# x1 transposed into the output, the last addition done onto it, and the sums and weight lows around it moved: one change to a streaming-encoder block

## The chip, the cores and the metric

The kernel runs on one core of a Trainium2 chip. The metric is the device time of one execution in microseconds (us). The kernel before was run three times: 2151.98, 2153.35 and 2154.61 us, median 2153.35. One further execution was recorded by the hardware profiler; its own time is 2155.38 us and the span from its first to its last instruction is 2153.6 us. The engines are called by the profile's names: PE is TensorE (PEld its weight loads), DVE is VectorE, ACT is ScalarE, POOL is GpSimd, SP is SyncE, which here only issues DMAs.

## The reference

One residual block over 2048 tokens of 1024 channels in float32, cut to what matters:

```python
h = rmsnorm(x, norm_mix_pre)
proj = h @ w_in                        # pool branch 512 | GLU 2*512 | gates 1024 + 1024
branch_a = pool_mixer(u_pool, ...)     # trailing means, per-group map, projection
branch_b = conformer_conv(u_glu, ...)  # GLU, causal depthwise conv, LayerNorm, swish, projection
merged = sigmoid(g_a) * branch_a + sigmoid(g_b) * branch_b
x = x + rmsnorm(merged @ w_o, norm_mix_post)          # called x1 below
h = rmsnorm(x, norm_mlp_pre)
f = square(relu(h @ w_up)) @ w_down                   # w_up 1024 x 4096, w_down 4096 x 1024
x = x + rmsnorm(f, norm_mlp_post)
# rmsnorm(x, g) = x * rsqrt(mean(x*x) + 1e-6) * g, over the 1024 channels of a token
```

The change lies in the last three lines and in what feeds them.

## The kernel before, in words

**Tiles and blocks.** The 2048 tokens are two blocks (b) of 1024, each of two halves (t) of 512 tokens. A half has four row groups (g) of 128 tokens. Almost every tile is 128 x 1024 float32, 512 KB. Up to the MLP's square, channels lie on the partitions and tokens along the row; x1 is stored in DRAM in that layout as tiles `x1d[b, c, t]` of two times 128 channels. The MLP's down projection turns this round: its results have tokens on the partitions and channels along the row, in two column halves of 512 (m).

**Products.** Each float32 operand is split into a high part (a cast on ACT) and a low part (source minus high, on DVE), and a product takes three passes, high x high, high x low and low x high. Matrix products are done in a scheme with seven products instead of eight, numbered 1 to 7, whose operands are sums and differences of quarters of the weights and of the activations. A `down` product for one number, one block and one row half h is 24 matmuls of 128 x 512 (line 1708).

**Stages.** Input projection, pooling and convolution branches, merge, output projection, then for each block the up products (`mlp_up`, eight octets), then the down products. The down stage goes over four slabs of the hidden dimension (s = 0 to 3), in each over the seven numbers and the two blocks: a job (s, i, b) is two products (h = 0, 1). Slabs 0 to 2 add into accumulators `acc`. In the last slab the order is: numbers 2, 1, 6, 7, 4 for both blocks, then 5 and 3 for block 0, then 5 and 3 for block 1, so that block 0 is done two jobs earlier. In the last four jobs each job brings its own weights.

**Order of the work.** TensorE's products are the main line. Everything else at its side runs in lanes: generators that are stepped by `bg()` once after each product (lines 1388 to 1420). A lane of rate r takes up to r steps per call; `yield n` makes the lane wait n calls. What a lane issues is ordered behind the main-line instruction last marked at that point. Weights and token cells are requested with a priority that puts them ahead of the main line. Each engine runs its instructions in a fixed order, so an instruction that waits holds back all behind it on that engine, DMA issues on SP and POOL too.

**What the change touches.**

- *Scale of the MLP's inner norm.* The second norm's factor never multiplies the up products; instead its square is folded into the epsilon of the last norm. That needs the mean square of x1 per token. `mlp_scale` (line 1312) computes it during block 1's up products: it loads the 16 tiles `x1d`, squares them on ACT, adds them on DVE, and sums over the partitions by small matmuls with one column (`root_acc`, line 458); `floor[b, t]` is the result.
- *Turning x1 round.* `turned` (line 1771) runs in the first three down slabs in a lane of rate 2: it loads quarters of x1 on POOL's queue, transposes 32 x 32 blocks on DVE (line 1785) and writes them, four DMAs of 128 KB each, into a DRAM tensor `x1t[b, t]` (tokens x channels).
- *Lows of the last slab's weights.* `last_weights` (line 1570) runs in the up stage: for all 14 weight tiles of the last slab it builds the sum or difference, stores the sums (`wsum`), splits them and stores the low parts (`lows`). In the last slab `weights_down(LAST)` (line 1609) loads a tile, casts the high part (line 1647) and loads the low part from `lows`, 18 times.
- *Finish.* `Finish` (line 1799) is one object per (b, t). As the four accumulators of a half become ready, `gain` takes their square sums on ACT (line 1812) and multiplies them by the norm's gain on DVE (line 126). When all are ready, `root` makes the factor r per token, `fetch` loads x1's rows from `x1t`, `cell` does x1 + r * y on DVE, two multiply-adds of 128 x 512 for each row group (line 1832), and `put` writes the row group to the output (line 1839). Three of the four halves do this in `steps`, one after the other in one lane. The last one, (1, 1), does its first half of columns in `last_steps` and the rest in `at_end`, called between the matmuls of the very last products (h = 0, then h = 1): `arrive` adds the product, takes squares and multiplies by the gain, and once both of a product's row groups have arrived, `leave` does the multiply-add with x1's rows and writes each half row (lines 1887 and 1888).

Of the kernel before, what the change touches and what calls it, by code (L numbers as in the profile page):

```python
# [15 lines left out]
P = 128  # L16
D = 1024
# [45 lines left out]
def f32(ap):  # L63
    return ap.bitcast(F32)
# [3 lines left out]
def block_kernel(  # L68
# [124 lines left out]
    fd, x1t = {}, {(b, t): dram("x1t", (T, D)) for b in range(NB) for t in (0, 1)}  # L193
# [958 lines left out]
    floor = {}  # L1152
# [158 lines left out]

    def mlp_scale(b, buf):

        st = None
        for t in (0, 1):
            sq = Squares(buf)
            for c in range(0, CPS, 2):
                x = [mk(*buf) for _ in (0, 1)]
                for i in (0, 1):
                    load(x[i], x1d[b, c + i, t])  # L1320
                yield 1
                sq.add(x[0])
                sq.add(x[1])
            yield 1
            ss = sq.total()
            yield 2
            if st is None:
                st = root_psum()
            root_acc(st, ss, inv_d, t * G)
        yield 1  # L1330
        m = small("sa", 2 * G)
        nc.vector.tensor_scalar(
            m, st[:, : 2 * G], EPS, SQ * EPS**0.5, op0=ALU.add, op1=ALU.mult
        )
        e = p_const.tile([P, 2 * G], F32, tag=f"e{b}", name=f"e{b}")
        mul(e, m, m)
        for t in (0, 1):
            floor[b, t] = e[:, t * G : (t + 1) * G]
        yield
# [230 lines left out]
    def last_weights():  # L1570
# [11 lines left out]
        keys = [(o, i) for o in (0, 1) for i in DOWN]  # L1582
        for (o, i), got in ahead_by_one(keys, fetch_one):
# [15 lines left out]
            hi, lo = split(t, *TR)  # L1599
            yield 1  # L1600
            lows[i, o] = dram("lows")
            load(lows[i, o], f32(lo))

    def scales():
        for b in range(NB):
            yield from mlp_scale(b, (p_fo, "fo"))


    def weights_down(s):
# [27 lines left out]
        def part(i, o):  # L1637
            with tc.high_priority(offset=AHEAD):
# [7 lines left out]
                hi, lo = mk(p_wh, "wh", F32R), mk(p_wl, "wl", F32R)  # L1646
                nc.scalar.copy(hi, t)
                load(f32(lo), lows[i, o])
                return hi, lo
# [120 lines left out]

    def turned():
        for b in range(NB):
            for t in (0, 1):
                to = x1t[b, t].rearrange("(n tb i) (q k j) -> n q i tb k j", n=2, i=32, q=4, j=32)
                for c in (0, 2):
                    for n in (0, 1):
# [7 lines left out]
                        yield 4  # L1784
# [9 lines left out]
                        yield  # L1794

# [3 lines left out]
    class Finish:  # L1799
# [254 lines left out]
```

## Time and profile before

| what | value |
|---|---|
| median of three runs | 2153.35 us |
| profiled execution | 2155.38 us, span 2153.6 us |
| mean granted TensorE clock | 0.996 |
| POOL busy | 74.8 us, 131 instructions |
| SP's queue | 490.93 MB, 63.4% of 16 engines' span |
| ACT's queue | 46.14 MB, 5.5% |
| POOL's queue | 29.37 MB, 3.9% |
| HBM read, written | 370.71 MB, 195.65 MB |

How to read the lines that follow. A row of the busy table by stage gives the stretch, its length, then for PE, PEld, DVE, ACT and POOL the busy us with the number of instructions in brackets, the granted clock, the DMA share and GB/s. A row of the wait table gives the engine and line, what it waited for, the total us, how often and the longest. A row of a group gives line, engine, operation, out<-in, shape and count, then busy us and the mean ns of one, then the idle time before them and its releasers. A row of the timeline gives start, duration, engine, line and operation; "x8" means eight merged. A DMA row gives the queue that issued, the count, the size of one and the median us from issue to landing. The DMA issues before that the change touches:

| transfer | queue | count | KB each | median us to landing |
|---|---|---|---|---|
| fo<-x1d (for the scale) | SP | 16 | 512 | 5.8 |
| tr<-x1d (to be turned) | POOL | 32 | 256 | 3.4 |
| x1t<-tr | POOL | 64 | 128 | 6.1 |
| big<-x1t | SP | 16 | 512 | 7.1 |
| fo<-w_down | SP | 18 | 512 | 6.7 |
| lows<-tr | SP | 14 | 512 | 5.3 |
| wl<-lows | SP | 18 | 512 | 5.2 |
| out<-big | SP | 4 | 512 | 5.0 |

### The profile page before, as it was taken

What the parts mean: (1) busy time and instruction counts of PE and PEld (TensorE: products, weight loads), DVE (VectorE), ACT (ScalarE), POOL (GpSimd) and SP (SyncE); (2) the same over time, 40 slices, a digit from 0 to 9 for tenths busy, and PEclk for the clock granted to TensorE, in tenths of its full rate; (3) what the DMA queues carried; (4) which work ended last, traced back from release to release, by engine and by line L of the source; (5) the groups of instructions that cost most, each with busy time, mean ns of one, the idle gap of its engine ahead of it and who ended that gap; (6) DMA issues with size and microseconds to landing.
All of it is one profiled execution on the core that took longest, in us unless ns stands there. A gap on an engine that the chain in (4) does not pass through costs nothing.

```text
span 2153.6 us, 24989 instructions
## 1 busy us (share of the span) xinstructions
PE 2130.3 (99%) x9424; PEld 1758.8 (82%) x9424; DVE 1717.0 (80%) x1669; ACT 1024.5 (48%) x1109; POOL 74.8 (3%) x131
## 2 busy tenths in 40 slices
PE   9999999999999999999999999999999999999997
PEld 8788888888888888888888888888888888888886
DVE  8999788999779999998768766876745667688558
ACT  6444453334534755446645676665544322223343
POOL 0000000000000000000000000000011111100000
PEclk9999999999999999999999999999999999999999
DMA  4789999688897787335596787995977657564568
GB/s 178 262 309 329 342 356 317 223 292 290 307 345 282 248 305 292 149 118 223 200 382 211 248 293 268 338 334 192 366 264 264 246 197 253 180 221 164 198 228 338
DMA packets 164617, 568.04 MB, mean 264 GB/s; under 512 B 19984, under 2 KB 24208, under 8 KB 164496
## 3 DMA queue, kind: packets, MB, share of 16 engines
q1 hardware_dynamic: 142736, 490.93, 63.4%
q10 hardware_dynamic: 12672, 46.14, 5.5%
q0 software_dynamic: 9088, 29.37, 3.9%
q8 instruction: 74, 1.21, 0.2%
q14 instruction: 47, 0.39, 0.1%
HBM read 370.71 MB, written 195.65 MB: 263 GB/s over the span
## 4 chain that ended last, share of the span: by engine, by line
PE 85%; DVE 8%; DMA 3%; issue 2%; ACT 1%; SPq 0%; DVEq 0%; ACTq 0%
PE up L252 28%; PE down L1708 26%; PE wo L252 7%; PE glu L252 4%; PE B L252 4%; PE gb L252 4%; PE A L252 4%; PE ga L252 3%; DVE y L910 3%; PE pool L252 3%; PE rb L1708 1%; DVE tr L120 1%; DVE wl L123 1%; DMA kept<-ws 1%; PE rb L458 1%
## 5 line engine op out<-in xcount | busy, mean ns | idle before, releaser
L252 PE MATMUL up<-big,wh 128*128 128x512 f32 x1792 | 481.0, 390 | 1.4 <-DVE big L123 0.8
L252 PEld LDWEIGHTS up<-big,wh 128*128 128x128 f32 x1792 | 335.7, 188 | 72.5 <-DVE big L123 1.1
L209 ACT CAST wh<-wr 128x1024 fp32r<-128x1024 f32 x167 | 175.6, 1052 | 305.8 <-PE up L252 70.0
L910 DVE SCALAR_TENSOR_TENSOR y<-v,cst,y 128x1024 f32<-128x1024 f32 x240 | 307.1, 1280 | 2.4
L1708 PE MATMUL down<-wh,fo 128*128 128x512 f32 x756 | 290.3, 389 | 0.3 <-DVE st L120 0.3
L1708 PE MATMUL down<-wh,tr 128*128 128x512 f32 x744 | 289.4, 389 | 0.0
L252 PE MATMUL up<-big,wl 128*128 128x512 f32 x896 | 276.0, 389 | 0.0
L209 ACT CAST wh<-ws 128x1024 fp32r<-128x1024 f32 x124 | 130.6, 1053 | 212.7 <-PE up L252 73.8
L1708 PE MATMUL down<-wl,fo 128*128 128x512 f32 x740 | 227.8, 389 | 0.0
L252 PEld LDWEIGHTS up<-big,wl 128*128 128x128 f32 x896 | 168.1, 188 | 35.0
L123 DVE TENSOR_TENSOR wl<-ws,wh 128x1024 fp32r<-128x1024 f32 x116 | 141.6, 1220 | 48.5 <-ACT wh L209 46.9
L1688 ACT CAST fo<-tr 128x1024 fp32r<-128x1024 f32 x86 | 89.9, 1052 | 176.8 <-DMA tr<-fd 121.0
L1708 PEld LDWEIGHTS down<-wh,fo 128*128 128x128 f32 x756 | 141.9, 188 | 30.4 <-issue 0.9
L1708 PEld LDWEIGHTS down<-wh,tr 128*128 128x128 f32 x744 | 139.6, 188 | 28.9
L1708 PEld LDWEIGHTS down<-wl,fo 128*128 128x128 f32 x740 | 138.9, 188 | 28.9
L123 DVE TENSOR_TENSOR wl<-wr,wh 128x1024 fp32r<-128x1024 f32 x111 | 135.2, 1219 | 25.6 <-ACT wh L209 22.6
L123 DVE TENSOR_TENSOR tr<-tr,fo 128x1024 fp32r<-128x1024 f32 x86 | 103.8, 1221 | 56.4 <-ACT fo L1688 55.9
L120 DVE TENSOR_TENSOR big<-big,down 128x1024 f32<-128x1024 f32 (+1 forms) x79 | 94.0, 1190 | 60.4 <-PE down L1708 60.0
L252 PE MATMUL gb<-big,wh 128*128 128x512 f32 x448 | 121.6, 393 | 0.0
L252 PE MATMUL glu<-big,wh 128*128 128x512 f32 x432 | 117.5, 393 | 3.2 <-ACT tr L408 3.2
L252 PE MATMUL wo<-big,wh 128*128 128x512 f32 x448 | 120.2, 390 | 0.0
L252 PE MATMUL ga<-big,wh 128*128 128x512 f32 x448 | 119.7, 389 | 0.0
(208 smaller groups left out, 3423.9 us busy)
## 6 DMA issues: line engine op xcount, KB each, us to landing
tr<-fd SPq DMA_DIRECT2D x110, 512.0 KB, 5.7
wl<-kept SPq DMA_DIRECT2D x67, 512.0 KB, 4.8
kept<-wl SPq DMA_DIRECT2D x66, 512.0 KB, 5.7
wr<-w_up SPq DMA_DIRECT2D x64, 512.0 KB, 4.6
wr<-w_down SPq DMA_DIRECT2D x62, 512.0 KB, 4.7
wr<-w_in SPq DMA_DIRECT2D x56, 512.0 KB, 5.6
fd<-tr ACTq DMA_DIRECT2D x54, 512.0 KB, 3.7
fd<-tr SPq DMA_DIRECT2D x48, 512.0 KB, 3.1
```

Of the source, the lines that this page charges most:

```text
L120: return nc.vector.tensor_tensor(o, a, b, op=ALU.add)
L123: return nc.vector.tensor_tensor(o, a, b, op=ALU.subtract)
L209: nc.scalar.copy(hi[:, :n], src[:, :n])
L252: i = nc.tensor.matmul(ps, w[wp][:, (at + k) * P : (at + k + 1) * P], rhs[k][xp], start=start and n == 0, stop=stop and n == len(order) - ...
L458: nc.tensor.matmul(st[:, at + g : at + g + 1], ss[:, g * P : (g + 1) * P], inv_n, start=start is None or (start and g == 0), stop=stop, sk ...
L910: nc.vector.scalar_tensor_tensor(acc, v[:, k : k + TB], wk, acc, op0=ALU.mult, op1=ALU.add)
L1688: nc.scalar.copy(hi, t)
L1708: i = nc.tensor.matmul(ps[gg], cells[j][xp][:, c * T + at : c * T + at + P], w[j][wp][:, c * T : (c + 1) * T], start=start and first, stop ...
```

## The change

Four edits. First, `x1t` is gone: `turned` writes x1 into the output tensor itself, at a quicker pace (lane rate 3, `yield 3`), and after each half it runs `row_squares`, which loads the half's rows back from the output (four tiles), squares them on ACT with a sum along the row, and makes the last norm's epsilon from the sums. `mlp_scale` and `scales` are gone. Second, `steps` no longer loads x1 or adds it: `over` multiplies two row groups of one column half by r and the gain in one DVE instruction each and sends both to the output by one accumulating DMA on POOL's queue. `gain` only takes square sums, but for the one accumulator that still needs the multiplication. Third, in `at_end` the product h = 0 (row groups 0 and 1) goes the same way, by two accumulating DMAs; the product h = 1 (row groups 2 and 3) still fetches x1 and writes the sum. Fourth, `last_weights` only makes the eight sums; the last slab's weights are split when they are loaded (`split_w`: cast on ACT, subtraction on DVE). The lane of the last half has rate 3 instead of 2, and the lags of the three halves' steps are 1, 0, 1 instead of 0, 1, 0.

```diff
-    fd, x1t = {}, {(b, t): dram("x1t", (T, D)) for b in range(NB) for t in (0, 1)}
+    fd = {}
...
-    def mlp_scale(b, buf):
...
-        keys = [(o, i) for o in (0, 1) for i in DOWN]
+        keys = [(o, i) for o in (0, 1) for i in DOWN if i in (5, 6, 3, 7)]
...
-            hi, lo = split(t, *TR)
-            yield 1
-            lows[i, o] = dram("lows")
-            load(lows[i, o], f32(lo))
...
-                hi, lo = mk(p_wh, "wh", F32R), mk(p_wl, "wl", F32R)
-                nc.scalar.copy(hi, t)
-                load(f32(lo), lows[i, o])
-                return hi, lo
+                return split_w(t)
...
+    def rows(b, t):
+        return out[b, t].rearrange("g p d -> (g p) d")
...
-                to = x1t[b, t].rearrange("(n tb i) (q k j) -> n q i tb k j", n=2, i=32, q=4, j=32)
+                to = rows(b, t).rearrange("(n tb i) (q k j) -> n q i tb k j", n=2, i=32, q=4, j=32)
...
-                        yield 4
+                        yield 3
...
+                yield 2
+                yield from fin[b, t].row_squares()
...
-            load(self.x[g], x1t[self.b, self.t][g * P : (g + 1) * P])
+            load(self.x[g], rows(self.b, self.t)[g * P : (g + 1) * P])
+
+        def row_squares(self):
+            sx = small("sx", G)
+            tiles = []
+            for g in range(G + 1):
+                if g < G:
+                    tiles.append(mk(*TR))
+                    load(tiles[g], rows(self.b, self.t)[g * P : (g + 1) * P])
+                    yield 1 + (g == 0)
+                if g:
+                    x = tiles[g - 1]
+                    nc.scalar.activation(x, x, AF.Square, accum_out=sx[:, g - 1 : g])
+            m = small("sm", G)
+            k = SQ * EPS**0.5
+            nc.vector.tensor_scalar(m, sx, k / D, k * EPS, op0=ALU.mult, op1=ALU.add)
+            self.floor = mk(p_gain, f"e{self.b}{self.t}", F32, (P, G))
+            mul(self.floor, m, m)
...
-            row = gains[0][:, m * T : (m + 1) * T].unsqueeze(1).to_broadcast([P, 2, T])
-            mul(two(y), two(y), row)
+            if self.b and self.t and h:
+                row = gains[0][:, m * T : (m + 1) * T].unsqueeze(1).to_broadcast([P, 2, T])
+                mul(two(y), two(y), row)
+
+        def over(self, m, h, r):
+            y, s = self.ready[m, h], slice(m * T, (m + 1) * T)
+            for gg in (0, 1):
+                part = y[:, gg * T : (gg + 1) * T]
+                nc.vector.scalar_tensor_tensor(
+                    part, part, r[:, gg : gg + 1], gains[0][:, s], op0=ALU.mult, op1=ALU.mult
+                )
+            to = out[self.b, self.t, 2 * h : 2 * h + 2].rearrange("g p d -> p g d")[:, :, s]
+            nc.gpsimd.dma_start(to, two(y), accum_op=ALU.add)
...
-            for g in range(3):
-                self.fetch(g)
             r = self.root(0, G)
             if lag:
                 yield lag
-            for g in range(G):
-                if g + 3 < G:
-                    self.fetch(g + 3)
-                self.cell(g, r[:, g : g + 1], self.parts(g))
-                self.put(g)
-                yield
+            for h in (0, 1):
+                for m in (0, 1):
+                    self.over(m, h, r[:, 2 * h : 2 * h + 2])
+                    yield
...
-                self.fetch(2 * n)
-                yield
-                self.fetch(2 * n + 1)
-                yield
+                if n:
+                    self.fetch(2 * n)
+                    yield
+                    self.fetch(2 * n + 1)
+                    yield
...
+            far = h == 0
...
-                mul(y[:, s], c[:, s], gains[0][:, :T])
+                if far:
+                    self.ready[0, h] = c
+                else:
+                    mul(y[:, s], c[:, s], gains[0][:, :T])
...
-                    if h:
+                    if far:
                         if gg:
-                            r = self.root(2, 4)
-                            for g in (2, 3):
-                                leave(g, r[:, g - 2 : g - 1])
+                            r = self.root(2 * h, 2 * h + 2)
+                            for m in (1, 0):
+                                self.over(m, h, r)
                     elif gg:
-                        r = self.root(0, 2)
-                        for g in (0, 1):
-                            leave(g, r[:, g : g + 1])
+                        r = self.root(2, 4)
+                        for g in (2, 3):
+                            leave(g, r[:, g - 2 : g - 1])
...
-    then(lambda: lanes.extend([Lane(1, scales()), Lane(1, last_weights())]), octs[1])
+    then(lambda: lanes.extend([Lane(1, last_weights())]), octs[1])
...
-                lanes += [Lane(3, fin[0, 0].steps(0), fin[1, 0].steps(1), fin[0, 1].steps(0)), Lane(2, fin[1, 1].last_steps())]
+                lanes += [Lane(3, fin[0, 0].steps(1), fin[1, 0].steps(0), fin[0, 1].steps(1)), Lane(3, fin[1, 1].last_steps())]
...
-            lanes.append(Lane(2, turned()))
+            lanes.append(Lane(3, turned()))
```

More of the change, by code (lines that the diff above doesn't have):

```diff
@@ L1825, in root @@
             add(ss, self.ss[:, lo:hi], self.ss[:, G + lo : G + hi])
[L1826 to L1841 removed]
+            return root_dve(ss, self.floor[:, lo:hi], 1.0 / D)
         def steps(self, lag):
```

45 lines of the change are left out of this document (1 added, 44 removed).

## The prediction

> **What bounds the kernel now.** I read the page's head and its busy shares first, then the busy time by stage, then TensorE's own waits, then the last 65 us engine by engine.
>
> ```profile
> span 2153.6 us, 24989 instructions
> PE 2130.3 (99%) x9424; PEld 1758.8 (82%) x9424; DVE 1717.0 (80%) x1669; ACT 1024.5 (48%) x1109; POOL 74.8 (3%) x131
> ```
>
> ```profile
> 1700.00:1800.00 100.00, 100.00 (x443) 82.80 (x442) 70.85 (x61) 29.75 (x29) 16.70 (x27) 1.00 0.68 234
> ...
> 2088.10:2099.00 10.90, 10.90 (x50) 9.03 (x49) 10.64 (x20) 10.34 (x23) 0.00 (x0) 1.00 0.85 310
> 2099.00:2109.90 10.90, 10.60 (x47) 8.44 (x47) 10.66 (x21) 4.15 (x9) 2.22 (x4) 1.00 1.02 383
> 2109.90:2120.80 10.90, 10.59 (x47) 8.44 (x46) 10.75 (x15) 5.04 (x10) 0.00 (x0) 1.00 1.01 403
> 2120.80:2131.70 10.90, 10.90 (x50) 9.03 (x49) 9.83 (x21) 3.95 (x9) 0.53 (x1) 1.00 0.91 329
> 2131.70:2142.60 10.90, 9.31 (x42) 7.37 (x40) 10.51 (x23) 4.24 (x12) 1.60 (x3) 1.00 1.00 369
> 2142.60:2153.50 10.90, 0.00 (x0) 0.00 (x0) 7.19 (x22) 0.10 (x2) 0.00 (x0) 0.52 0.56 213
> ```
>
> The stage rows give the stretch, its length, then the busy time of PE, PEld, DVE, ACT and POOL, the granted clock, the DMA share and GB/s. TensorE is the bound: it is full in the middle of the down stage (100.00 of 100) while ScalarE works 30 of 100. There only what TensorE itself executes, or is made to wait for, counts. The last 65 us are different. VectorE is busy for 10.64, 10.66, 10.75, 9.83 and 10.51 of 10.9 us, the DMA engines are at 0.85 to 1.02, and after the last matmul there are about 12 us without TensorE. So the end has two bounds in turn: TensorE to about 2141, then VectorE.
>
> TensorE's own waits from 1300 us on are these two, 0.6 us together:
>
> ```profile
> PE down L1708 <- DMA wl<-lows: 0.3, 1, 0.3
> PE down L1708 <- DVE st L120: 0.3, 1, 0.3
> ```
>
> Nothing else in the second half of the kernel can be won on TensorE except by giving it less to do.
>
> **Part 1: the MLP scale's sums (mlp_scale leaves, row_squares comes).** The old sums end in small matmuls on line 458, in the middle of the up products:
>
> ```profile
> L458 PE MATMUL rb<-inv_d,fo x32: 164/250/270, 1341.4 to 1445.1; 128*128 128x1 f32 x32
> 1341.44 0.95 PE L458 MATMUL rb<-inv_d,fo 128*128 128x1 f32 x8
> 1342.24 1.65 PE L252 MATMUL up<-big,wh 128*128 128x512 f32 x6
> ```
>
> ```profile
> 1444.26 1.05 PE L458 MATMUL rb<-inv_d,fo 128*128 128x1 f32 x8
> 1445.17 0.71 PE L252 MATMUL up<-big,wh 128*128 128x512 f32 x2
> ```
>
> 32 records are four groups of eight (two blocks, two halves). The first group pushes the next product back by 1342.24 - 1341.44 = 0.80 us, the last by 0.91. Four groups at 0.80 to 0.91 are 3.2 to 3.6; I take 3.3. TensorE is full on both sides, so all of it comes off the end: **-3.3 us**. The 16 loads, 16 ScalarE squares and VectorE additions beside them were hidden and are worth nothing.
>
> In their place 16 row loads of 512 KB and 16 squares run in the down stage, where ScalarE has 70 of 100 us free. The first of them sits behind the transposing writes, so a new wait stands on SP, with weight and token loads queued behind it, then ScalarE's casts, then TensorE. Such a wait exists already, between 1540 and 1980:
>
> ```profile
> SPq L129 <- DMA x1t<-tr: 6.9, 1, 6.9
> 2090.84 5.44 PE rb L1708 x24
> ```
>
> It held SP for 6.9 us and cost TensorE nothing. A product is 5.44 us and a job has two, so tokens and weights loaded a job ahead have 10.9 us of lead. Cost: 0; if that lead is gone, up to 6.9 us for each of four waits. The quicker pace of the transposition (three background steps instead of four) moves the same transfers earlier and is covered by the same full TensorE.
>
> **Part 2: the last slab's weight lows are computed.** 18 loads go, and 18 subtractions on VectorE come; in the up stage the 14 splits and 14 stores that made them go, hidden there, worth nothing.
>
> ```profile
> wl<-lows SPq DMA_DIRECT2D x17, 512.0 KB, 5.5
> L1647 ACT CAST wh<-wr 128x1024 fp32r<-128x1024 f32 x15 | 15.8, 1052 | 33.1 <-PE rb L1708 21.1 <-PE down L1708 12.0
> L123 DVE TENSOR_TENSOR tr<-tr,big 128x1024 fp32r<-128x1024 f32 x3 | 3.6, 1217 | 0.0
> 2099.66 5.38 DVE L1832 SCALAR_TENSOR_TENSOR big<-big,sy,big 128x512 f32<-128x512 f32 x8
> ```
>
> A load took 5.5 us, a cast of the high part 1.05, a subtraction of the same shape 1.22. There are three buffers of a kind and two in use, so in the four last jobs, which each bring new weights, the second weight of a job waits for a buffer that comes free in the middle of the second product before (2.72 us before the job begins). TensorE needs its low part 2.72 + 4 x 0.23 = 3.6 us after the job begins. That is 6.3 us for 1.05 + 1.22, so 4.1 us of slack; in the last job, which takes its halves in another order, 2.7. A run of eight multiply-adds (5.38) put in front of the subtraction would therefore cost TensorE 1.3 us, in the last job 2.7. If all four jobs met one: 3 x 1.3 + 2.7 = 6.6 us. The other end is a gain of 0.3, the wait for lows above. I take 0: the load that leaves took longer (5.5) than cast and subtraction together (2.3) and cost only 0.3, and VectorE as a whole gets lighter here (part 3).
>
> **Part 3: the last step.** The multiplication by the gain is folded into the multiply-add, which no longer adds x1; the addition is done by accumulating DMAs. VectorE from 2088 us to the end, grouped:
>
> ```profile
> L126 DVE TENSOR_TENSOR big<-big,ws 128x1024 f32<-128x1024 f32 x11 | 13.3, 1221 | 1.9 <-ACT ws L1812 1.9
> L1832 DVE SCALAR_TENSOR_TENSOR big<-big,sy,big 128x512 f32<-128x512 f32 x24 | 16.6, 745 | 0.1
> L126 DVE TENSOR_TENSOR tr<-big,ws 128x512 f32<-128x512 f32 x4 | 2.7, 685 | 0.0
> ```
>
> Of the eleven gain multiplications one stays (the last block's second half of rows): 10 x 1.22 = 12.2 us go. Two of the four half-size ones go: 1.4. The 24 multiply-adds stay 24, with another operand, at the same 0.75. About seven of the 18 subtractions fall in here: 7 x 1.22 = 8.5. Net -5.1 us of 59.
>
> What that is worth at the end is read from VectorE's last instructions:
>
> ```profile
> 2141.20 0.68 DVE L120 TENSOR_TENSOR big<-big,rb 128x512 f32<-128x512 f32 x1
> ...
> 2143.19 0.75 DVE L1887 SCALAR_TENSOR_TENSOR big<-big,sy,big 128x512 f32<-128x512 f32 x1
> ...
> 2145.85 0.16 DVE L499 TENSOR_SCALAR sy<-sa 128x2 int32<-128x2 int32 x1
> ...
> 2147.42 0.75 DVE L1887 SCALAR_TENSOR_TENSOR big<-big,sy,big 128x512 f32<-128x512 f32 x1
> ...
> 2149.41 0.75 DVE L1887 SCALAR_TENSOR_TENSOR big<-tr,sy,big 128x512 f32<-128x512 f32 x1
> ```
>
> The last product's sum is added at 2141.20. Its root is begun when four multiply-adds of the first row groups, late from the backlog, come in between: they run from 2143.19 to 2145.85, and only then does the root of the last groups go on. Without them it would have gone on up to 2145.85 - 2143.19 = 2.7 us earlier. These four are as many after the change, so they must run earlier; the 5.1 us that VectorE loses make room before 2141, in part while it waits for TensorE. At the least the two half-size multiplications just ahead are won, of which some 0.6 falls on the chain. Between 0.6 and 2.7, nearer the upper as the room (5.1) is almost twice the block: **-2.0 us**.
>
> The first two row groups now leave by two accumulating DMAs, which no row of this trace shows. Nearest rows, plain writes:
>
> ```profile
> out<-big POOLq DMA_DIRECT2D x8, 512.0 KB, 8.1
> out<-big SPq DMA_DIRECT2D x8, 256.0 KB, 2.1
> 1552.57 1.77 POOL L133 DMA_DIRECT2D x1t<-tr  x3 [13.12 <-DVE tr L1785]
> 1558.75 0.59 POOL L133 DMA_DIRECT2D x1t<-tr  x1 [4.41 <-DMA wr<-w_down]
> ```
>
> 512 KB from POOL landed in 8.1 us with the engines full, 256 KB from SP in 2.1 at the end, when they are half idle; so 512 KB there lies between 2.1 and 8.1 (4.2 if two such writes follow one another). An accumulate may cost as much, or twice that. On today's clock the second would be issued when the block ends, 2145.85 - 2.0 = 2143.9. Today the last write is issued at 2150.2 (0.75 after 2149.41), lands 2.1 later at 2152.3, and the span ends at 2153.6, 1.3 after that. Moved up by 2.0 the last landing is 2150.3, so an accumulate is hidden up to 2150.3 - 2143.9 = 6.4 us. The last slab moves less than today (14 of 16 tiles of x1 are no longer fetched, nor 18 lows, 512 KB each), so I take some 5 us, between the ends and nearer to neither, hidden, and nothing added. POOL can hold back a fourth DMA of 256 pieces (4.41 us in the row above); an accumulate has 256 pieces too, but behind it on POOL there are only accumulates.
>
> The Trainium skill, "DMA: Bandwidth & Descriptors", section on the anatomy of a SWDGE DMA, gives such a POOL transfer about 2.0 us plus its bytes over 436 GB/s, an estimate of 3.2 us here; the 8.1 of the row disagrees, since the engines are full, and the sum would be the same by either.
>
> **The sum.** 3.3 + 0 + 2.0 = 5.3 us less: the profiled execution (2155.38, of which the span is 2153.6) would be 2150.1, and the median of the runs, 2153.35, becomes **2148.0**. About 0.2%, or 4.3 us, is what a measurement here can tell from no change; the forecast lies just beyond it.
>
> **Rival A: lows late.** TensorE waits for subtractions behind runs of multiply-adds. For it: VectorE at 96% (52.4 of the first five rows' 54.5 us) and four spaces of only 2.7 to 4.1 us. Against: the earlier slabs split weights in this way at 100.00 of 100. Half of the worst (6.6) is +3.3: 2151.3, no change by the bound.
>
> **Rival B: the accumulates set the end.** Each costs twice the plain write: from 2 x 4.2 (twice two SP writes of 256 KB) to 2 x 8.1 us. The second lands at 2143.9 + 8.4 = 2152.3 to 2160.1; with 1.3 behind it and 3.3 ahead the span ends at 2150.3 to 2158.1, the time (0.25 under the span, as 2153.35 to 2153.6) is 2150.1 to 2157.9, in the middle 2154.0. For it: nothing else in the tail is new. Against it: the engines are half idle there. In the Trainium skill, "Collectives: The Full Stack", part 3 (why ReduceScatter is half of AllGather) says that the sum itself is free but a reduce has two source reads on one ring and so runs at half a copy's rate. No run here shows it; by it this rival's doubling is right, and its size then hangs on the load.
>
> **Rival C: slower.** The accumulates run one after the other, each waiting for the one before.
>
> ```profile
> 2128.64 4.07 DVE L1832 SCALAR_TENSOR_TENSOR big<-big,sy,big 128x512 f32<-128x512 f32 x6
> ```
>
> The third part's multiply-adds begin there, so its first accumulate goes out at about 2130. Its four and the two of the last part at 8.1 each end at 2178.6, so the span at 2176.6: 2176.3, slower. It decides from 5.0 us each: (2153.6 + 4.3 + 3.3 - 1.3 - 2130) / 6. Against: three POOL writes to one tensor went out in 1.77 us without a wait. That the change does nothing is no case of its own: the 32 small matmuls leave in any event, so at the least 3.3 us do.
>
> **How the numbers follow.** Forecast 0.60, own range 2146.5 to 2150; A 0.18, B 0.14, C 0.08. The low end is the forecast with everything: 2153.35 - 3.3 - 0.6 - 2.7 = 2146.7, less about 0.9 for the spread of the runs (2151.98 to 2154.61): 2145.8. The high end takes in A nearly to its worst (2148.0 + 6.6 = 2154.6) and the lower half of B: 2154.0; left out are C, half of B and the ends of the others. Faster by over 0.2% (under 2149.05): most of the forecast's range and a little of A, 0.55. Slower (over 2157.65): C and the far end of B, 0.10. Same: 0.35.
>
> **What would show it.** Right: no line 458 matmul between 1300 and 1500; TensorE still 100.00 in every stretch to 2080; its waits under 1 us; the last root running through without a block of multiply-adds; the end set by a 256 KB write from SP. Wrong: TensorE waiting for VectorE's lows (A); the last landing a POOL accumulate (B); POOL issues each starting as the one before lands (C); or SP held by row loads for more than 10.9 us and TensorE idle behind it.

## The result, and the profile after

The kernel after takes 2193.33 us (median of four runs, 2192.71 to 2194.67); the kernel before, run beside it, 2153.98 (four runs, 2151.98 to 2158.7). The ratio is 1.0179, with a 95% interval of 1.0165 to 1.0192: slower by some 39 us, where 5.3 us less were forecast. The profiled execution's span grew by the same, from 2153.6 to 2192.9.

The head of the page of the kernel after, and its busy shares:

```profile
span 2192.9 us, 24799 instructions
PE 2127.4 (97%) x9392; PEld 1755.3 (80%) x9392; DVE 1690.2 (77%) x1646; ACT 1014.1 (46%) x1111; POOL 87.3 (4%) x137
```

The 32 small matmuls are gone (9424 to 9392), TensorE and VectorE work less than before, and yet the span is longer. So it is not work that grew. The busy time by stage says where (stretch, length, then PE, PEld, DVE, ACT, POOL, granted clock, DMA share, GB/s), in the stretches shown of before and one more:

```profile
1700.00:1800.00 100.00, 96.64 (x423) 78.73 (x422) 68.26 (x61) 33.77 (x37) 12.71 (x20) 1.00 0.69 246
...
2099.00:2109.90 10.90, 10.90 (x49) 9.01 (x48) 10.55 (x22) 5.76 (x12) 1.22 (x1) 1.00 1.02 277
2109.90:2120.80 10.90, 10.90 (x50) 9.01 (x49) 9.36 (x12) 4.92 (x11) 2.40 (x2) 1.00 0.43 59
...
2131.70:2142.60 10.90, 10.56 (x47) 8.43 (x45) 8.94 (x22) 3.62 (x10) 2.40 (x2) 1.00 0.54 61
2142.60:2153.50 10.90, 0.00 (x0) 0.00 (x0) 7.14 (x19) 0.72 (x2) 2.22 (x2) 0.66 0.78 170
2153.50:2192.80 39.30, 0.00 (x0) 0.00 (x0) 0.00 (x0) 0.00 (x0) 6.23 (x6) 0.50 0.61 83
```

Up to 2142.60 the end looks as before, only with lighter VectorE rows. Then comes a stretch of 39.30 us that has no counterpart before: four engines do nothing, and POOL issues six DMAs. The first row shows a second, smaller loss: 96.64 of 100 where TensorE was full.

POOL's timeline from 2085 us on, six of the 14 accumulating DMAs (start, duration, and in brackets POOL's idle time before with its releaser):

```profile
2096.70 1.25 POOL L1812 DMA_DIRECT2D out<-big  x1 [153.60 <-DVE big L1808]
2103.49 1.22 POOL L1812 DMA_DIRECT2D out<-big  x1 [5.54 <-DVE big L120]
...
2125.80 1.20 POOL L1812 DMA_DIRECT2D out<-big  x1 [5.47 <-DVE sy L504]
...
2139.26 1.20 POOL L1812 DMA_DIRECT2D out<-big  x1 [5.54 <-DVE s L126]
...
2178.49 1.21 POOL L1812 DMA_DIRECT2D out<-big  x1 [5.48 <-issue]
2185.15 1.21 POOL L1812 DMA_DIRECT2D out<-big  x1 [5.46 <-issue]
```

And their row among the DMA issues after 2080 us (queue, count, KB each, median us from issue to landing), with the one of the four last writes from SP:

```profile
out<-big POOLq DMA_DIRECT2D x14, 512.0 KB, 6.3
out<-big SPq DMA_DIRECT2D x4, 256.0 KB, 4.5
```

An accumulate lands 6.3 us after its issue, and the next is issued some 0.3 us after that: 2178.49 + 6.3 = 2184.8, and the next starts at 2185.15. After the first, the idle time before each is 5.1 to 5.5 us, but for the third (7.81), whether the page blames VectorE's sums, a root, or nothing ("issue"). An idle time that hardly changes while its releaser does is unlikely to have any of them as its cause. The last lands at 2185.15 + 6.3 = 2191.5, and the span ends 1.4 us later.

That the data were ready long before is seen on VectorE's timeline:

```profile
2141.36 2.74 DVE L1808 SCALAR_TENSOR_TENSOR big<-big,sy,ws 128x512 f32<-128x512 f32 x4
2144.02 0.68 DVE L120 TENSOR_TENSOR big<-big,rb 128x512 f32<-128x512 f32 x1
...
2145.55 0.16 DVE L120 TENSOR_TENSOR st<-ss 128x2 f32<-128x2 f32 x1
...
2147.31 0.16 DVE L504 SCALAR_TENSOR_TENSOR sy<-s,sy 128x2 f32<-128x2 f32 x1
2147.51 0.75 DVE L1864 SCALAR_TENSOR_TENSOR big<-big,sy,big 128x512 f32<-128x512 f32 x1
...
2149.50 0.74 DVE L1864 SCALAR_TENSOR_TENSOR big<-tr,sy,big 128x512 f32<-128x512 f32 x1
```

The multiplications for the last two accumulates (L1808: the former multiply-adds, which now multiply by r and by the gain) end at 2144.1; the last of the two goes out 41 us later. The same rows show the tail as the prediction wanted it: the block of four now runs before the last product's sum, and the last root goes through without a break.

TensorE's waits from 1300 us on, where there were 0.6 us before:

```profile
PE down L1666 <- DVE tr L123: 3.4, 4, 1.5
PE down L1666 <- DVE big L120: 0.3, 1, 0.3
```

So two things were to be explained: the row of accumulates (39 us), and 3.4 us of waits that took the place of the 3.3 us of small matmuls.

### The profile page after: what moved, and what is told of

It reads as the page before. It is cut to its first block, busy times and chain, and to the rows that moved or that the text cites. A ratio compares the mean times of both kernels' runs of the same rounds, so it can differ in the third digit from the quotient of the medians.

```text
span 2192.9 us, 24799 instructions
## 1 busy us (share of the span) xinstructions
PE 2127.4 (97%) x9392; PEld 1755.3 (80%) x9392; DVE 1690.2 (77%) x1646; ACT 1014.1 (46%) x1111; POOL 87.3 (4%) x137
## 3 DMA queue, kind: packets, MB, share of 16 engines
q8 instruction: 74, 1.21, 0.2%
## 4 chain that ended last, share of the span: by engine, by line
PE 69%; issue 13%; DVE 11%; DMA 4%; ACT 1%; POOL 1%; SPq 1%; POOLq 0%; DVEq 0%; ACTq 0%
PE up L252 27%; PE down L1666 16%; PE wo L252 7%; DVE y L910 4%; PE B L252 4%; PE gb L252 3%; PE ga L252 3%; PE glu L252 3%; PE A L252 2%; PE pool L252 2%; DVE wl L123 1%; DVE tr L120 1%; DMA kept<-wl 1%; DVE tr L123 1%; DMA big<-xt 1%
## 5 line engine op out<-in xcount | busy, mean ns | idle before, releaser
L209 ACT CAST wh<-wr 128x1024 fp32r<-128x1024 f32 x185 | 194.7, 1053 | 387.5 <-PE up L252 90.3
L123 DVE TENSOR_TENSOR wl<-wr,wh 128x1024 fp32r<-128x1024 f32 x129 | 157.0, 1218 | 39.2 <-ACT wh L209 37.2
L120 DVE TENSOR_TENSOR big<-big,down 128x1024 f32<-128x1024 f32 (+1 forms) x79 | 93.9, 1189 | 83.6 <-PE down L1666 83.4
```

What stands on the lines that cost most here:

```text
L120: return nc.vector.tensor_tensor(o, a, b, op=ALU.add)
L123: return nc.vector.tensor_tensor(o, a, b, op=ALU.subtract)
L209: nc.scalar.copy(hi[:, :n], src[:, :n])
```

## The experiments

**The theories.** RING: POOL writes the descriptors of a DMA (the records that say which piece goes where; a piece is a run of bytes that lie together) into a space that the program reserves (1024 bytes on each partition, its dynamic_dma_scratch_size), and an accumulate needs so much of it that only one fits; POOL waits until the one before has landed. A first rival, ORDER: DMAs into one tensor are put one after the other, by the program or the queue, whatever they do. A second, ENGINE: accumulates as such are done one at a time, whatever their size. A third, by load: the accumulates are slow because the DMA engines are full. In the built program an accumulate waits for a semaphore of the POOL transfer eight before it, not of the one before, so the program at least does not order them; and against the load speaks the DMA share of 0.61 in the last 39.30 us.

RING has an arithmetic, an estimate. The Trainium skill, "DMA: Bandwidth & Descriptors", calls a descriptor a 16-byte structure (section on the terms), and has one pair of them, for the read and for the write, put into rings for each piece (section on SWDGE, HWDGE and iDMA). 1024 / 16 = 64 places; a transfer of 256 pieces puts 256 / 16 = 16 and one to finish on each of 16 DMA engines, so 17: three fit (51), a fourth doesn't (68). The Trainium skill, "Collectives: The Full Stack", part 3, gives a reduce two source reads; then an accumulate of 256 pieces takes 33: one fits, a second (66) doesn't. The trace agrees in both counts (three plain ones and a held fourth in the prediction's rows, one accumulate here); the places themselves no run shows, nor the second read. The packets that the traces count do not stand for places: an accumulate made 3808 / 14 = 272 = 16 x 17 of them, a plain write of the same shape 2016 / 14 = 144 (run plain), but one of x1t's plain writes before, of which a fourth was held back, only 48 (POOL's queue from 1500 to 2000: 5632 = 32 loads x 80 + 64 writes x 48).

### plain: plain writes in place of the accumulates

```diff
-            nc.gpsimd.dma_start(to, two(y), accum_op=ALU.add)
+            nc.gpsimd.dma_start(to, two(y))
```

> The 14 last-step DMAs of the changed kernel on POOL's queue, same shape (256 pieces of 2 KB), but plain writes: x1 is overwritten and so not added. Theory RING (the space for POOL's descriptors lets only one accumulate be under way, since an accumulate takes twice the room of a plain transfer with as many pieces, of which three went out together before): plain ones go out up to three together, the queue is no longer behind, and the end is set by VectorE and the last SP writes: 2150 to 2155 us. Theory ENGINE (accumulates as such are done one at a time): the same 2150 to 2155. Theory ORDER (each DMA into the output waits for the one before, whatever it does): spacing stays at 5 us or more, 14 x 5 from 2097, and the time is 2168 to 2185.

2153.71 us, ratio 0.9998 (0.9986 to 1.001). POOL's group of this line (count, busy us, mean ns, idle time before and its releasers), first in the kernel after, then in plain:

```profile
L1812 POOL DMA_DIRECT2D out<-big x14 | 16.9, 1208 | 226.3 <-DVE big L1808 153.6 <-issue 37.5 <-DVE big L120 18.9
L1812 POOL DMA_DIRECT2D out<-big x14 | 10.1, 719 | 192.3 <-DVE big L1808 192.3
```

And the DMA rows after 2080 us:

```profile
out<-big POOLq DMA_DIRECT2D x14, 512.0 KB, 3.5
out<-big SPq DMA_DIRECT2D x4, 256.0 KB, 2.1
```

All of POOL's idle time is now put down to the multiplications (L1808): each write goes out when its data are there. So it is not ORDER, and the whole 39 us belong to the adding itself; RING and ENGINE both allow that. And what is left of the change, without the adding, is worth nothing that can be measured: the forecast's -5.3 is not there either.

### halves: each accumulate as two of 128 pieces

```diff
-            nc.gpsimd.dma_start(to, two(y), accum_op=ALU.add)
+            for gg in (0, 1):
+                nc.gpsimd.dma_start(to[:, gg], two(y)[:, gg], accum_op=ALU.add)
```

> Each accumulate of 512 KB split into two of 256 KB (128 pieces of 2 KB), 28 in all; bytes and pieces as in the changed kernel. RING: half the room each, so three are under way at a time; the DMA engines' own time for the pieces (16 x 0.24 us per accumulate of 512 KB, 14 of them, 54 us from 2097) becomes the limit: 2152 to 2165 us. ENGINE and ORDER: one at a time, each with its fixed part, 28 x 4 us or more: 2205 us or more.

2158.58 us, ratio 1.0014 (1.0003 to 1.0026). POOL's timeline begins so:

```profile
2092.53 2.75 POOL L1813 DMA_DIRECT2D out<-big  x3 [152.89 <-DVE big L1808]
```

The DMA row of all 28:

```profile
out<-big POOLq DMA_DIRECT2D x28, 256.0 KB, 5.2
```

Three go out without a wait between them, each still 5 us from landing. The same bytes in the same pieces to the same places, added in the same way, and nearly all of the loss is gone. ORDER or ENGINE would have kept them apart. POOL is still held now and then: of its 181.3 us of idle time before this line, 159.0 are put down to the multiplications, the other 22.3 to several other releasers or none, as RING would have it where a fourth doesn't fit.

### rowgroups: accumulates of 128 pieces of 4 KB

The multiplications write a whole row group into a new tile, and one accumulate of 512 KB adds it in whole rows:

```diff
...
-            to = out[self.b, self.t, 2 * h : 2 * h + 2].rearrange("g p d -> p g d")[:, :, s]
-            nc.gpsimd.dma_start(to, two(y), accum_op=ALU.add)
+            nc.gpsimd.dma_start(out[self.b, self.t, g], o, accum_op=ALU.add)
...
```

> The multiply-adds write a whole row group into one tile, and the accumulates go by row group: 14 of 512 KB as before, but 128 pieces of 4 KB. RING: room for three at a time, 2152 to 2165 us, the nearer to 2152 the more the engines' time goes by pieces and not by bytes. ENGINE and ORDER: still one at a time, 2185 to 2195 us.

2156.15 us, ratio 1.0002 (0.999 to 1.0013). POOL's group of the line:

```profile
L1812 POOL DMA_DIRECT2D out<-big x14 | 12.3, 875 | 189.4 <-DVE big L1809 186.5 <-DVE big L120 2.9
```

The DMA rows after 2080 us:

```profile
out<-big POOLq DMA_DIRECT2D x14, 512.0 KB, 8.5
out<-big SPq DMA_DIRECT2D x4, 256.0 KB, 5.1
```

POOL waits for its data again, not for a landing, with the same 512 KB in each accumulate: it is the pieces that count, not the bytes. An accumulate now takes longer to land (8.5 against 6.3), now that several are under way at once. And the four last writes from SP take 5.1 us instead of 2.1.

### ring5k and wr4: five times the room, and its control

The room comes out of the memory of a pool of weight tiles, so the control takes that tile away alone.

```diff
-    p_wr = pool("pwr", 5)
+    p_wr = pool("pwr", 4)                      # both
-    ... dynamic_dma_scratch_size=1024)
+    ... dynamic_dma_scratch_size=5120)         # ring5k alone
```

> The changed kernel with five times the space for POOL's descriptors (5120 bytes a partition instead of 1024); to make room the raw weights have four buffers instead of five, which may cost TensorE up to some 5 us. RING: seven accumulates of the same shape fit, so the queue is bound by the engines' time: 2152 to 2167 us. ENGINE and ORDER: nothing changes in the tail, 2190 us or more.

> The control for ring5k: the changed kernel with four buffers for raw weights instead of five and the old 1024 bytes of space for POOL's descriptors. RING: TensorE as late as in ring5k (its first accumulate went out at 2114.5, 18 us after that of the changed kernel), and behind it the full one-at-a-time queue of 14 x 6.5 us: about 2210 us. If instead the four buffers cost nothing, it ends at 2193 as the changed kernel does.

ring5k took 2179.86 us (two runs), ratio 1.0113 (1.0063 to 1.0164), span 2173.6; wr4 2220.23 in one run, span 2218.5. POOL's first accumulate and its group of the line in ring5k:

```profile
2114.49 1.24 POOL L1812 DMA_DIRECT2D out<-big  x1 [154.66 <-DVE big L1808]
L1812 POOL DMA_DIRECT2D out<-big x14 | 16.8, 1197 | 187.2 <-DVE big L1808 186.1 <-issue 1.1
```

And in wr4 the first accumulate and one of the last on POOL's timeline:

```profile
2121.94 1.25 POOL L1812 DMA_DIRECT2D out<-big  x1 [153.69 <-DVE big L1808]
...
2191.05 1.21 POOL L1812 DMA_DIRECT2D out<-big  x1 [5.53 <-issue]
```

With the instructions of the kernel after unchanged, the room alone takes POOL's waits away and 2218.5 - 2173.6 = 44.9 us off the span. Of these, 2121.94 - 2114.49 = 7.5 us lie ahead of the first accumulate and are not the queue's. From the first accumulate to the end of the span it is 96.6 us in wr4 and 96.2 in the kernel after, but 59.1 in ring5k, near the 56.8 of plain. This is what RING says and no rival does. RING's range for the time, 2152 to 2167, was missed, since four weight buffers cost more than the 5 us it allowed: the first accumulate goes out 18 us (ring5k) and 25 us (wr4) later than in the kernel after. So it is no remedy here, and ring5k stays slower than the kernel before.

### rg_lastload: no accumulate in the last half

As rowgroups, but the last half of the last block fetches x1 and adds it on VectorE, as in the kernel before.

```diff
-            if self.b and self.t and h:
+            if self.b and self.t:
...
-            far = h == 0
+            far = False
...
```

> Accumulates by row group (as in rowgroups) for three of the four halves; the last half fetches x1 and writes as the kernel before does, so no accumulate is issued in the last 10 us. In rowgroups the four last writes from SP landed in 5.1 us instead of 2.1, beside two accumulates. Theory CONTENTION: they land in 2.1 again, the tail is some 2 to 3 us shorter than that of rowgroups: 2150 to 2153. Theory VECTOR (the tail is VectorE's work, which is now longer by two half-size multiplications): no gain, 2154 to 2157.

2154.26 us, ratio 0.9997 (0.9985 to 1.0009). The DMA row of SP's last writes:

```profile
out<-big SPq DMA_DIRECT2D x8, 256.0 KB, 2.1
```

The last writes take 2.1 us again: it was the accumulates beside them that made them 4.5 to 5.1. From TensorE's last matmuls to the end it is 2150.0 - 2137.16 = 12.8 us, in rowgroups 2155.0 - 2140.08 = 14.9, so the tail is shorter, as CONTENTION said. The median of the runs lies in VECTOR's range, but the runs spread from 2149.98 to 2159.51, wider than what separates the two. This is the quickest correct version here, and it takes as long as the kernel before.

### lows_only: part 2 by itself

The kernel before, with the last slab's lows computed (18 subtractions) and 14 splits and stores fewer in the up stage; the multiplications by the gain stay.

```diff
...
-                hi, lo = mk(p_wh, "wh", F32R), mk(p_wl, "wl", F32R)
-                nc.scalar.copy(hi, t)
-                load(f32(lo), lows[i, o])
-                return hi, lo
+                return split_w(t)
```

> The kernel before with one part of the change: the last slab's lows computed on VectorE instead of loaded. With the gain multiplications still in place VectorE has some seven subtractions (8.5 us) more in its full last 65 us. Theory LATE (rival A of the prediction): waits for lows of 1 to 3 us in the last four jobs and a tail some 2 to 5 us longer: 2156 to 2160. Theory HIDDEN: within 1 us of before.

2173.93 us, ratio 1.0086 (1.0069 to 1.0103). TensorE's waits from 1100 us on:

```profile
PE rb L458 <- DVE fo L120: 6.0, 2, 5.5
PE down L1701 <- DVE st L120: 6.0, 1, 6.0
PE up L252 <- ACT tr L408: 2.0, 2, 1.8
PE down L1701 <- DVE big L120: 1.1, 1, 1.1
```

15.1 us of waits, hardly any of them there before, in two places; both theories expected less. In the last slab TensorE waits for VectorE, 6.0 + 1.1 us, a little over rival A's worst case (6.6). It is rival A's crowding, but not its wait for lows: the 6.0 us stand before a matmul of the high weights, and what VectorE finished just ahead, behind a row of other work, was the addition of an earlier product (L120 at 2126.42). In the up stage TensorE waits for the sums of the MLP scale (line 458). The likely reason, which no run here isolates, is that the lane with the weights has become shorter and the sums no longer come in time. In the kernel after neither is left (0.3 us in the whole down stage on L120): the folded gain frees VectorE, and the sums are gone.

### scale_only and pace_only: part 1 by itself, and its pace alone

scale_only is the kernel before with the row sums in place of mlp_scale, and the quicker turning round. pace_only has nothing but the pace:

```diff
-                        yield 4
+                        yield 3
...
-            lanes.append(Lane(2, turned()))
+            lanes.append(Lane(3, turned()))
```

> The kernel before with one part of the change: mlp_scale gone, row_squares in its place (reading x1's rows from the separate tensor), turned at the quicker pace. Theory ROWS (the row loads and squares in the down stage cost TensorE what the 32 small matmuls gave): 3.3 us less to do, about 3.4 us of waits for token lows between 1700 and 1800, net within 1 us of before. Theory OTHER (those waits come from another part, such as the writes into the output): no such waits, 3.3 us less than before.

> The kernel before with nothing changed but the pace of turned (three background steps instead of four, lane rate 3). Theory PACE (the quicker transposition puts TensorE's waits for token lows between 1700 and 1800 there): the same waits, about 3.4 us in all. Theory ROWS (the row loads and squares put them there): none, TensorE's waits after 1300 stay at 0.6 us and the time is that of before.

scale_only: 2157.1 us, ratio 1.0006 (0.9993 to 1.0019), TensorE's main wait from 1100 us on:

```profile
PE down L1708 <- DVE tr L123: 4.0, 5, 1.5
```

Its stage row:

```profile
1650.00:2000.00 350.00, 346.08 (x1521) 284.88 (x1520) 250.91 (x223) 126.35 (x137) 43.87 (x70) 1.00 0.65 229
```

The small matmuls are gone, and TensorE loses 350 - 346.08 = 3.9 us in the down stage: the gain is given back there. pace_only, in one run, took 2165.61 us and lost 350 - 343.75 = 6.3 us in the same stretch. Its main wait:

```profile
PE down L1708 <- ACT fo L1688: 5.3, 2, 2.7
```

So the quicker pace alone makes TensorE wait for casts of tokens on ScalarE. These waits end at 1652.03 and 1690.27, though, while the two long ones of the kernel after, of which more below, end at 1706.88 and 1796.17: the loss is of the same kind, but the waits are not the same ones.

### rg_later, rg_slow, rg_aside: where the 3.4 us come from

All three are rg_lastload with one thing moved: the row sums after all four halves are turned; the old number of steps (4) with the row loads two by two; the row loads on POOL's queue instead of SP's.

```diff
...
-                    load(tiles[g], rows(self.b, self.t)[g * P : (g + 1) * P])
+                    aside(tiles[g], rows(self.b, self.t)[g * P : (g + 1) * P])    # rg_aside
...
```

> rg_lastload with the row loads and squares of all four halves after the last transposition, instead of after each half's. ROWS: the waits move to where the squares now run, or go if the token tiles then have room; at best 3.4 us less than rg_lastload, 2150 to 2151 beside 2154.9 of before. PACE: the waits between 1700 and 1800 stay.

> rg_lastload with the old pace of the transposition (yield 4, lane rate 3) and the row loads two at a time with one background step between, so that it still ends before the last slab. PACE: no waits between 1700 and 1800, 3.4 us less than rg_lastload: 2150 to 2151 beside 2154.9 of before. ROWS: waits of 2 us or more remain in the down stage, 2152 to 2155.

> rg_lastload with the row loads issued on POOL's queue instead of SP's. If the waits for token lows come from SP being held by row loads (their wait for the transposing writes, or the extra transfers in its queue), they go, 2150 to 2151. If they come from the four-tile hold on the token buffers or from ScalarE standing at a square, they stay: 2153 to 2155.

rg_later: 2163.32 us, 1.0034 (1.0023 to 1.0046), worse, with 350 - 342.51 = 7.5 us lost. rg_slow: 2157.04, 1.0007 (0.9994 to 1.002). rg_aside: 2155.99, 1.0 (0.999 to 1.001). TensorE's largest wait in rg_later:

```profile
PE down L1666 <- ACT fo L1646: 6.2, 2, 3.5
```

And in rg_aside:

```profile
PE down L1666 <- DVE tr L123: 3.4, 4, 1.5
```

rg_slow has two rows of 1.9 us. None takes the waits away. With the row loads off SP the wait is the same to the tenth, so it is not SP that is held, which the prediction had among its signs.

### rg_pace and rg_keepscale: the old pace, and the old sums

rg_pace is rg_lastload with the old pace and the row sums; rg_keepscale has the old pace and the old mlp_scale, so that only the computed lows, the folded gain and the accumulates by row group, onto x1 in the output, are left of the change.

```diff
-                        yield 3
+                        yield 4
...
-            lanes.append(Lane(3, turned()))
+            lanes.append(Lane(2, turned()))
```

> Accumulates by row group, the last half fetched, and the transposition at the pace of the kernel before (four steps, its lane at 2), row sums kept. If it is the quicker pace that costs the 3.4 us of waits for token casts (as the run with the pace alone said), they shrink under 1 us and the time is 3 us under that of rg_lastload: ratio 0.9983. If the row sums' own loads cost them, 3 us or more of waits stay and the ratio is 0.9997 or above. Rival: the lane now ends too late, and the last step's roots wait for row sums: waits of VectorE or a late first accumulate after 2080, ratio over 1.000.

> As rg_pace, but with the sums of the MLP scale as in the kernel before (32 small matmuls in the up stage) and no row sums: what is left of the change are the computed lows, the folded gain, and accumulates by row group. If row sums and pace together only moved the 3.3 us from the small matmuls to waits, its span is that of rg_lastload within 1 us (2150), ratio 0.9983 to 1.000, with 32 matmuls at L458 and under 1 us of waits in the down stage. If the shorter work in the up stage (14 splits and stores fewer) makes the sums late, as with the lows alone, some 6 us of waits stand at the up products: ratio 1.002.

Both are slower: rg_pace 2170.7 us, 1.0072 (1.0051 to 1.0093); rg_keepscale 2164.88, 1.0053 (1.0036 to 1.007). In rg_pace the lane now reaches into the last slab, and ScalarE's timeline there shows the mechanism at its plainest:

```profile
2005.04 1.06 ACT L1783 ACTIVATE tr<-tr 128x1024 f32<-128x1024 f32 x1 [13.45 <-DMA tr<-out]
...
2013.29 1.04 ACT L1646 CAST fo<-tr 128x1024 fp32r<-128x1024 f32 x1
```

and TensorE's at the same place:

```profile
2001.22 0.61 PE L1666 MATMUL down<-wl,fo 128*128 128x512 f32 x2
2014.39 0.80 PE L1666 MATMUL down<-wh,fo 128*128 128x512 f32 x1 [12.56 <-ACT fo L1646]
```

ScalarE stands for 13.45 us before the square of a row tile whose load hasn't come. The cast of the next product's tokens stands behind it on the same engine; it runs only when the four squares are done, and TensorE has stood still for 12.56 us. In the kernel after ScalarE also waits before squares, for shorter times; two rows of its table for ScalarE between 1500 and 2050:

```profile
ACT wh L209 <- PE down L1666: 121.5, 37, 17.8
ACT tr L1783 <- DMA tr<-out: 23.3, 7, 5.2
```

The squares' waits are new (23.3 us). Casts of weights waiting for a buffer that TensorE has yet to free take 121.5 us, where the same row of the kernel before has 53.8 us. It is these, and not squares, that stand ahead of TensorE's two longest waits in the kernel after, as ScalarE's and TensorE's timelines show:

```profile
1698.85 1.05 ACT L209 CAST wh<-ws 128x1024 fp32r<-128x1024 f32 x1 [10.40 <-PE down L1666]
1706.88 0.50 PE L1666 MATMUL down<-wh,tr 128*128 128x512 f32 x1 [1.53 <-DVE tr L123]
...
1788.14 1.05 ACT L209 CAST wh<-wr 128x1024 fp32r<-128x1024 f32 x1 [17.81 <-PE down L1666]
1796.17 0.50 PE L1666 MATMUL down<-wh,tr 128*128 128x512 f32 x1 [1.52 <-DVE tr L123]
```

ScalarE stands for 10.40 and 17.81 us before a weight cast; the token casts come bunched behind it, and VectorE's subtractions, for which TensorE waits, behind them. Between each pair of rows no square runs. This is read from the order on each engine; no run moves the weight casts.

Without row sums, at the old pace, rg_keepscale loses only 350 - 348.86 = 1.1 us in this stretch, but 200 - 196.75 = 3.3 in the up stage (1300 to 1500), where the old sums meet the shorter lane as in lows_only. TensorE's waits there:

```profile
PE up L252 <- ACT tr L408: 2.0, 2, 1.8
PE rb L458 <- DVE fo L120: 1.4, 1, 1.4
```

## Why the prediction was wrong

**The failed step is part 3: "some 5 us, between the ends and nearer to neither, hidden, and nothing added".** It costed one accumulate as the last of two and asked whether it would land within 6.4 us. It does, nearly to the number: 6.3. But it cannot be issued when its data are there, because it is the fourteenth of a row in which each waits for the one before: 88.5 us from the first issue (2096.70) to the last (2185.15), 6.8 on the average. Shown by halves, rowgroups, and ring5k against wr4: where more than one fits, the row and its 39 us all but disappear. Of the prediction's own signs of being wrong, the one for rival C came: each issue starts as the one before lands.

**Rival C had the outcome and the order, without a cause and at a wrong count.** It took 8.1 us each and only six, from 2130 on, and came to 2176.3. Each took 6.8, but by 2130 only five had gone out, where plain had sent eleven. With 14 from 2096.7 the same sum gives 2096.7 + 13 x 6.8 + 6.3 + 1.4 = 2192.8. It was given 0.08 on the argument that "three POOL writes to one tensor went out in 1.77 us without a wait". Those were plain writes; the row just below, in which a fourth was held back for 4.41 us, was the one to work with. It was put aside since "behind it on POOL there are only accumulates", when accumulates were just what would be held. Three fit and four do not; a transfer with twice the descriptors fits once, as two would be four. Rival B quoted the doubling and applied it to the duration alone, not to the room.

**Rival B** had a true part: the adding does cost time beside others. SP's last writes take 4.5 to 5.1 us with accumulates under way and 2.1 without. It is hidden behind the row in the kernel after, and is worth some 2 us at the end of rowgroups (14.9 against 12.8).

**Part 1: -3.3 was right, "Cost: 0" was not.** The matmuls left, and 3.4 us of waits came (scale_only: 4.0). The prediction looked for the new wait on SP and gave it 10.9 us of lead. It starts on ScalarE, which it had counted as free because it is idle 70 of 100 us. Idle is not the same as free on an engine that runs in order: whatever waits there holds the token casts behind it. In rg_pace that is a square; in the kernel after, at the two longest waits (3.1 of the 3.4 us), a weight cast. Why the weight casts come to stand there, through the row sums or the quicker pace, stays open: the pace alone lost 6.3 us in its one run, and the three ways of moving the row sums gave no less than 3.4.

**Part 2: 0 was right in the whole, for half of the reason given.** "VectorE as a whole gets lighter here" carries it. Without that, the step costs 7.1 us in the last slab, and as much again in the up stage, where the prediction called the leaving splits "hidden there, worth nothing": without them the old sums come late. Parts 1, 2 and 3 pay for one another.

**The tail: -2.0 was too much.** The root runs unbroken, as forecast. From TensorE's last matmul to the end of the span before took 2153.6 - 2140.39 = 13.2 us; plain takes 2148.8 - 2136.95 = 11.9. That is -1.3, in the range of 0.6 to 2.7, but below its middle.

Put together, -3.3 + 3.7 (350 - 346.33, TensorE's idle time between 1650 and 2000) - 1.3 = -0.9 us for all but the adding. plain measured 2153.71 against 2155.16 beside it, a ratio of 0.9998 (0.9986 to 1.001). So even without the row of accumulates the change would have been no change.

## What to carry to other kernels

Before moving work to POOL's DMAs, count not how long one takes but how many can be under way: find in the trace the row where POOL holds back the next transfer, count the pieces that fit, and count an accumulate's pieces twice. Split or reshape transfers until several fit (fewer, longer pieces), or give the descriptors more room if it costs nothing else. And when an instruction with a new wait is put on an engine that is mostly idle, ask what stands behind it there: an in-order engine at 30% can stop TensorE.

## What the runs showed of the hardware

- An accumulating DMA of 512 KB in 256 pieces landed in 6.3 us alone, a plain one of the same shape in 3.5. The Trainium skill, "DMA: Bandwidth & Descriptors", section on the anatomy of a SWDGE DMA, gives an estimate of 3.2 us for a POOL transfer of this size; the plain one's 3.5 is near it, the accumulate's 6.3 is not.
- Its issue occupies POOL for 1.21 us (16.9 / 14), the plain one's 0.72.
- One at a time, accumulates kept the DMA engines at 0.61 over 39.30 us for six, so, as an estimate, 0.61 x 39.3 / 6 = 4.0 us of all 16 engines each. Overlapping could win no more than the idle 0.39, and with several under way the landings grew to 8.5 (rowgroups) and 9.2 us (ring5k).
- After its idle 12.56 us in rg_pace TensorE ran slower for a while: the matmuls from 2016.24 on come every 0.43 us, where before the wait and from 2021.26 on they come every 0.23. The granted clock is 0.51 between 2014.4 and 2021.3 and 1.00 from there to 2050. The 14 matmuls from 2014.39 to 2021.26 took 6.9 us, where 14 x 0.23 = 3.2 would do and 0.5 is a further wait. So the long wait cost some 3 us beyond its own length.
